# Decoder layer on one core: the two output projections of a chunk in one run of segments, layer-norm sums taken in the residual's addition, pools in another order

## The chip, the cores and the metric

One NeuronCore of a Trainium2 chip runs the whole layer in one launch. The metric is the device time in microseconds (us) of that core, median over runs; less is better. TensorE (PE), VectorE (DVE), ScalarE (ACT), GpSimd (POOL) and SyncE (SP) each execute their own instructions in order. In this program SP issues every DMA.

## The reference

One layer of a decoder, sequence 2048, width 1024, float32. What matters of it here:

```
shift, scale, gate = silu(c) W_ada + b_ada
h = x * (1 + scale) + shift
[q k v | g_attn | u B C | g_conv | m_attn m_conv] = h W_in
A: 3 dilated causal head groups, 4 heads x 128 each, merged per head by
   softmax denominators;      a = (o * silu(g_attn)) W_attn_out
B: s = (B * conv3_causal(C * u) * silu(g_conv)) W_conv_out
y = (sigmoid(m_attn) * a + sigmoid(m_conv) * s) W_o
out = LayerNorm(alpha * x + (1 + gate) * y)        # eps 1e-5, gain, bias
```

## The kernel before

Every product is a float32 product in three matmuls: each operand is split into a high and a low part (ACT casts the high part, L517; DVE subtracts it, L518), and hi·hi, lo·hi and hi·lo are added in one PSUM bank.

**Stage 1** computes the combined projection by Strassen-Winograd block products of seven (L617 to L619), the gates, the short convolution, and writes q, k, gates (`sg_scr`) and the convolution's rows (`y_scr`) to DRAM.

**Stage 2** (`attention_stage`) is a list of segments that a small look-ahead runner (`run_segs`) works through: weights are loaded five segments ahead and split three ahead. Groups g = 1 and 2 come first, then group 0 over four chunks of 512 tokens. In a chunk c of group 0 there are the V products and heads, the merges of the three groups for the four heads (`merge`, L449 to L458, all on DVE: a head's output times a broadcast weight, plus two other groups' outputs times theirs, times a gate; three `ab`, two `og` and one `gt` loads each), `co_segs(c)` (the convolution's output projection: eight segments of 24 matmuls; gate load L318, multiplication L319, store to `pa_scr` L320), and `ao_segs(c - 1)` (the attention's output projection: eight segments of 12 matmuls; gate load L332, load of the stored product L333, multiplication L334, addition L335, store to `mg_scr` L336). `ao_segs(3)` ends the stage. Three PSUM banks (`mm`) hold the products of V and of both projections, so that PE's fourth product in a row waits until DVE has emptied a bank. Both gates' tiles, `sg`, are one pool name with two buffers.

**Stage 3** loads `w_o`, multiplies it by the gate row (L987), forms the seven combinations (T rows), and runs eight steps of two 128-token blocks: load, combine and split the block (L600 to L610, L517, L518), seven products (p1 to p7, 12 matmuls each), and in `put` the residual and the layer norm: addition L1006, `alpha * x` added L1007, an ACT pass for the mean L1012, an ACT pass for the squares L1013, a power on POOL L1015, scaling L1017, gain on DVE L1018, bias on POOL L1019.

The order of the instructions on each engine is decided by a scheduler at build time; waits are put where tiles are shared. Pools are stacked: a pool's memory is reused by a later pool, and the first use waits for what was there.

Of the kernel before, what the change touches and what calls it, by code (L numbers as in the profile page):

```python
# [11 lines left out]
F32 = mybir.dt.float32  # L12
F32R = mybir.dt.float32r
# [19 lines left out]
LAG = 384  # L33
W_Q, W_K, W_G, W_U, W_B, W_C, W_GC, W_MA, W_MC = 0, 12, 24, 28, 36, 44, 52, 60, 68
# [19 lines left out]
def attention_stage(tc, psum1, wp, hp, kq, pa, pm, split, ident, scp, mod, w_v, w_ao, w_co, xm, xn,  # L54
                    qk_scr, nb_scr, ga_scr, o_scr, st_scr, st0_scr, al_scr, om_scr, y_scr, sg_scr, pa_scr, mg_scr):
# [90 lines left out]
    def classes_of(t):  # L146
        return t.rearrange("p (a r) -> p r a", r=4)

    nb = [[kq.tile([P, P if g == 2 else 256], F32, name=f"nb{g % 2}{j}" if g < 2 else f"nb{g}{j}")
           for j in range(NH)] for g in range(3)]  # L150

    def load_nb(g):
        for j in range(NH):
            SP.dma_start(nb[g][j], nb_scr[g, j, :, :256 if g < 2 else P])
# [157 lines left out]
    def co_segs(c):  # L312

        ys, at = [], slice((c % 2) * CH, (c % 2 + 1) * CH)
        for d in range(KT):
            def coseg(i, unit, d=d):
                sg = pm.tile([P, CH], F32, name="sg", bufs=2)
                SP.dma_start(sg, sg_scr[c // 2, 1, d, :, at])  # L318
                V.tensor_mul(sg, sg, gemm(unit, ys))  # L319
                SP.dma_start(pa_scr[c // 2, d, :, at], sg)  # L320
            seg([w_co[d]], coseg, prep_rows([y_scr[c // 2, k, :, at] for k in range(KT)], ys) if d == 0 else None)

    def ao_segs(c):

        os_, at, box = [], slice((c % 2) * CH, (c % 2 + 1) * CH), {}
        for d in range(KT):
            def aoseg(i, *units, d=d):
                if units:
                    box["u"] = units[0]
                sg = pm.tile([P, CH], F32, name="sg", bufs=2)  # L330
                co = pm.tile([P, CH], F32, name="co", bufs=2)
                SP.dma_start(sg, sg_scr[c // 2, 0, d, :, at])  # L332
# [5 lines left out]
            seg([w_ao[d // 2]] if d % 2 == 0 else [], aoseg,  # L338
                prep_rows([om_scr[c, :, j, :] for j in range(NH)], os_) if d == 0 else None)
# [59 lines left out]
    for c in range(NCH):  # L399
# [5 lines left out]
        def done(j, ps, c=c, st=st, o0=o0, box=box):  # L405
# [11 lines left out]
            for g in (1, 2):  # L417
                raw = pm.tile([NH * 4, 2, P], F32, name="alr", bufs=2)
# [52 lines left out]
    for g in (1, 2, 0):  # L471
        load_nb(g)
# [4 lines left out]
def layer_kernel(ctx: ExitStack, tc: tile.TileContext, x, xm, xn, cvec, wada, bada, w_main, w_v,  # L477
# [35 lines left out]
    pa_scr = dram.tile([2, KT, P, PAIR], F32, name="pa_scr")  # L513
# [9 lines left out]
    @contextmanager  # L523
    def block_products():

        with ExitStack() as s:
            rooms["ps"] = s.enter_context(tc.tile_pool(name="psum2", bufs=1, space=bass.MemoryType.PSUM,
                                                       reuse_waits="tile"))
            rooms["work"] = s.enter_context(tc.tile_pool(name="work", bufs=1, reuse_waits="tile"))
            rooms["t"] = s.enter_context(tc.tile_pool(name="tp", bufs=1, reuse_waits="tile"))  # L530
            rooms["s"] = s
            yield rooms["work"]

    def t_pool(i):

        if i < 3:
            return rooms["t"]
        if rooms.get("s3") is not rooms["s"]:
            rooms["s3"] = rooms["s"]
            rooms["t3"] = rooms["s"].enter_context(tc.tile_pool(name="tp3", bufs=1, reuse_waits="tile"))  # L540
        return rooms["t3"]
# [4 lines left out]
    def big():  # L546
        return rooms["work"].tile([P, PAIR + 64], F32, name="big", bufs=4)

    def row():
        return rooms["work"].tile([P, DM], F32, name="row", bufs=2)  # L550

    def half():
        return rooms["work"].tile([P, CH], F32, name="t", bufs=7)

    def raw_tile():
        return rooms["work"].tile([P, DM], F32, name="raw", bufs=3)

    def t_split(T, p, i, src):
        hi = t_pool(i).tile([P, CH], F32R, name=f"th{p}{i}")
        lo = t_pool(i).tile([P, CH], F32R, name=f"tl{p}{i}")  # L560
        split(hi, lo, src)
        T[p, i] = (hi, lo)
# [213 lines left out]
    with block_products() as w:  # L776
# [4 lines left out]
        with tc.tile_pool(name="ada", bufs=1, reuse_waits="tile") as ada:  # L781
# [26 lines left out]
            first_h(3)(xa, xb)  # L808
        t_row(T, 3, xa, xb)
# [151 lines left out]
    with ExitStack() as stage:  # L961
# [3 lines left out]
        wp, hp, kq, pa, pm = (pool(n) for n in ("wp", "hp", "kq", "pa", "pm"))  # L965
        attention_stage(tc, psum1, wp, hp, kq, pa, pm, split, ident, scp, mod, w_v, w_ao, w_co, xm, xn,
                        qk_scr, nb_scr, ga_scr, o_scr, st_scr, st0_scr, al_scr, om_scr, y_scr, sg_scr, pa_scr, mg_scr)

    w = ctx.enter_context(block_products())
# [4 lines left out]
    def load_w(i):  # L974
        def load(xa, xb):
            if i == 0:
                gate_row = rows_["gate"] = row()
                for hh in range(2):
                    pg = ps_bank()
                    for k in range(4):  # L980
                        PE.transpose(pg[:, k * P:(k + 1) * P],
                                     mod[:, 2, hh * 4 + k:hh * 4 + k + 1].to_broadcast([P, P]), ident)
                    S.copy(gate_row[:, hh * CH:(hh + 1) * CH], pg)
# [11 lines left out]
    for tb in range(0, SEQ // P, 2):  # L995
        def norm(tb=tb):
            zs = [big()[:, :DM] for _ in range(2)]

            def put(k, hh, last):
                def f(r, bank):  # L1000
                    z = zs[k]
# [5 lines left out]
                    V.scalar_tensor_tensor(z[:, hs], xr, ALPHA, z[:, hs], op0=ALU.mult, op1=ALU.add)  # L1007
# [6 lines left out]
                    V.tensor_scalar(mv[:, 1:2], mv[:, 1:2], 1.0 / DM, LN_EPS, op0=ALU.mult, op1=ALU.add)  # L1014
# [69 lines left out]
```

## Time and profile before

| | |
|---|---|
| runs | 2724.41, 2720.09, 2718.11 us; median 2720.09 |
| the profiled execution | 2715.16 us, of which the span of the profile is 2713.4 |
| PE busy | 2482.0 us (91%) |
| DVE busy | 1721.0 us (63%) |
| ACT, POOL busy | 1057.3 us (39%), 74.1 us (3%) |
| mean granted TensorE clock | 0.96 of full speed |

Stage 1 lies at 0 to 1533.6 us, groups 1 and 2 at 1533.6 to 1916, group 0 with the projections at 1916 to 2452, stage 3 at 2452 to 2713.4. The busy shares are means over stages with different limits; what a stage loses is read from its waits and its clock, in the rows below.

### The profile page before, as it was taken

How to read it: one execution, taken by the hardware profiler on the slowest of the kernel's cores; microseconds unless marked ns; L12 is line 12 of the kernel's file. 1: busy time of each engine (PE TensorE's matmuls, PEld its weight loads, DVE VectorE, ACT ScalarE, POOL GpSimd, SP SyncE). 2: the span in 40 equal slices, each digit the busy share in tenths (PEclk: the TensorE clock that was granted, in tenths of full speed). 3: DMA queues.
4: the chain of work that ended last, by engine and by line, in shares of the span. 5: the costliest groups of instructions: out<-in, count | busy, mean ns of one | idle time of the engine just before them, and what ended most of it. 6: DMA issues, size and time to landing. Idle time of an engine off the chain costs nothing.

```text
span 2713.4 us, 32007 instructions
## 1 busy us (share of the span) xinstructions
PE 2482.0 (91%) x11878; PEld 2102.1 (77%) x11878; DVE 1721.0 (63%) x2787; ACT 1057.3 (39%) x1741; POOL 74.1 (3%) x46
## 2 busy tenths in 40 slices
PE   3999999999989999999999799999999697956786
PEld 2778888888877888888888699999987586844664
DVE  8745566676667555676655346545677767658665
ACT  5323333333453223333333345554635243303444
POOL 2000000000000000000000000000000000000232
PEclk8999999999999999999999899999999898978888
DMA  6333322212443323122122455544578878675332
GB/s 237 121 111 128 113 70 78 70 67 97 148 163 104 122 101 117 63 70 77 63 101 94 145 150 152 150 116 136 174 245 265 265 244 270 213 241 172 113 117 100
DMA packets 205769, 378.73 MB, mean 140 GB/s; under 512 B 22653, under 2 KB 93484, under 8 KB 205612
## 3 DMA queue, kind: packets, MB, share of 16 engines
q1 hardware_dynamic: 205612, 376.68, 43.2%
q8 instruction: 93, 1.52, 0.2%
q14 instruction: 64, 0.52, 0.1%
HBM read 282.71 MB, written 93.90 MB: 139 GB/s over the span
## 4 chain that ended last, share of the span: by engine, by line
PE 70%; DMA 11%; DVE 9%; issue 6%; ACT 2%; POOL 1%; SPq 1%; POOLq 0%; DVEq 0%; ACTq 0%
PE pb L617 17%; PE pb L619 17%; PE pb L618 17%; PE mm L139 5%; PE mm L140 5%; PE mm L141 5%; DMA sg<-sg_scr 2%; DVE tl L518 1%; DMA ab<-al_scr 1%; DMA og<-o_scr 1%; DMA mg_scr<-sg 1%; DMA xs<-in_xn 1%; PE pt L221 1%; POOL big L1019 1%; DMA kr<-qk_scr 1%
## 5 line engine op out<-in xcount | busy, mean ns | idle before, releaser
L617 PE MATMUL pb<-th,w2h 128*128 128x512 f32 x2016 | 800.0, 399 | 84.0 <-ACT th L517 58.6
L618 PE MATMUL pb<-tl,w2h 128*128 128x512 f32 x2016 | 799.3, 397 | 9.9 <-DVE tl L518 9.8
L619 PE MATMUL pb<-th,w2l 128*128 128x512 f32 x2016 | 797.1, 397 | 12.0 <-DVE w2l L518 12.0
L617 PEld LDWEIGHTS pb<-th,w2h 128*128 128x128 f32 x2016 | 385.7, 191 | 180.6 <-ACT th L517 68.1
L618 PEld LDWEIGHTS pb<-tl,w2h 128*128 128x128 f32 x2016 | 386.2, 192 | 100.4 <-DVE tl L518 20.4
L619 PEld LDWEIGHTS pb<-th,w2l 128*128 128x128 f32 x2016 | 386.8, 192 | 96.1 <-DVE w2l L518 16.0
L517 ACT CAST w2h<-raw 128x1024 fp32r<-128x1024 f32 x168 | 176.7, 1052 | 345.6 <-PE pb L618 285.9
L518 DVE TENSOR_TENSOR w2l<-raw,w2h 128x1024 fp32r<-128x1024 f32 x168 | 214.2, 1275 | 150.0 <-ACT w2h L517 149.8
L626 ACT COPY t<-pb 128x512 f32<-128x512 f32 x248 | 144.3, 584 | 367.7 <-PE pb L619 363.5
L139 PE MATMUL mm<-whi,hhi 128*128 128x256 f32 x768 | 250.6, 327 | 19.4 <-ACT hhi L517 15.9
L141 PE MATMUL mm<-whi,hlo 128*128 128x256 f32 x768 | 247.2, 324 | 2.6 <-DVE hlo L518 2.6
L140 PE MATMUL mm<-wlo,hhi 128*128 128x256 f32 x768 | 248.4, 324 | 0.0
L139 PEld LDWEIGHTS mm<-whi,hhi 128*128 128x128 f32 x768 | 184.9, 241 | 21.3 <-ACT hhi L517 17.4
L139 PE MATMUL mm<-hhi,whi 128*128 128x512 f32 x384 | 158.4, 413 | 45.4 <-DVE sg L334 43.1
L141 PEld LDWEIGHTS mm<-whi,hlo 128*128 128x128 f32 x768 | 184.1, 241 | 3.2 <-DVE hlo L518 3.2
L140 PEld LDWEIGHTS mm<-wlo,hhi 128*128 128x128 f32 x768 | 185.3, 241 | 0.1
L517 ACT CAST whi<-raw 128x1024 fp32r<-128x1024 f32 x96 | 100.6, 1048 | 168.9 <-PE mm L140 70.9
L518 DVE TENSOR_TENSOR wlo<-raw,whi 128x1024 fp32r<-128x1024 f32 x96 | 116.9, 1219 | 69.8 <-ACT whi L517 69.5
L140 PE MATMUL mm<-hlo,whi 128*128 128x512 f32 x384 | 155.4, 405 | 0.2 <-DVE hlo L518 0.2
L141 PE MATMUL mm<-hhi,wlo 128*128 128x512 f32 x384 | 155.3, 405 | 0.0
L517 ACT CAST w2h<-xs 128x1024 fp32r<-128x1024 f32 x84 | 88.6, 1055 | 132.8 <-PE pb L618 114.4
L617 PE MATMUL pb<-th,w1h 128*128 128x512 f32 x336 | 132.6, 395 | 3.5 <-DVE big L1006 3.0
(169 smaller groups left out, 3421.4 us busy)
## 6 DMA issues: line engine op xcount, KB each, us to landing
raw<-in_w_main SPq DMA_DIRECT2D x152, 512.0 KB
qk_scr<-big SPq DMA_DIRECT2D x48, 512.0 KB
raw<-in_w_v SPq DMA_DIRECT2D x48, 512.0 KB
sg_scr<-big SPq DMA_DIRECT2D x32, 512.0 KB
sg<-sg_scr SPq DMA_DIRECT2D x64, 256.0 KB
raw<-in_w_co SPq DMA_DIRECT2D x32, 512.0 KB
qr<-qk_scr SPq DMA_DIRECT2D x48, 256.0 KB
ab<-al_scr SPq DMA_DIRECT2D x48, 256.0 KB
```

Source lines behind the costliest of these rows:

```text
L139: PE.matmul(o, a[0], b[0], start=start, stop=False)
L140: PE.matmul(o, a[0], b[1], start=False, stop=False)
L141: PE.matmul(o, a[1], b[0], start=False, stop=stop)
L221: PE.transpose(ps[:, n * P:(n + 1) * P], P_t[b][:, a:a + P], ident)
L517: S.copy(hi, src)
L518: V.tensor_sub(lo, src, hi.bitcast(F32))
L617: PE.matmul(bank, a[0], b[0], start=start, stop=False, **kw)
L618: PE.matmul(bank, a[0], b[1], start=False, stop=False, **kw)
L619: PE.matmul(bank, a[1], b[0], start=False, stop=stop, **kw)
L626: S.copy(r, bank)
L1019: G.tensor_add(z, z, rows_["b"])
```

## The change

- `out_segs(c)` takes the place of `co_segs` and `ao_segs`: the segments of both projections of one chunk are interleaved, attention's output tile d three behind the convolution's (`LATE = 3`). The convolution's gated product stays in its tile (`sg1`, five buffers) until it is added; `pa_scr` and its 64 transfers are gone. Each gate has its own tile name. `out_segs(c - 1)` follows chunk c's V and heads; `out_segs(3)` ends the stage, so that `out_segs(2)` and `out_segs(3)` are one run.
- Merges come two to a segment. `alr` has one buffer. Group 0's bias tiles share those of group 1 and are loaded later.
- The norm's mean comes from an addition that also sums its row (L1014); the ACT pass for the mean is dropped; the square pass is in two halves, into `half()` tiles; the gate row is scaled by 1/alpha so that x is added unscaled.
- Stage 2's pools are entered as wp, hp, pm, kq, pa, and stage 3's as s, T rows 1 to 3, T row 0, prep.

```diff
-    def co_segs(c):
...
-                V.tensor_mul(sg, sg, gemm(unit, ys))
-                SP.dma_start(pa_scr[c // 2, d, :, at], sg)
...
-    def ao_segs(c):
...
-                SP.dma_start(co, pa_scr[c // 2, d, :, at])
...
+    def out_segs(c):
+        os_, ys, at, box, late = [], [], slice((c % 2) * CH, (c % 2 + 1) * CH), {}, []
         for d in range(KT):
+            def gate(which, d=d):
+                sg = pm.tile([P, CH], F32, name=f"sg{which}", bufs=LATE + 2 if which else 2)
+                SP.dma_start(sg, sg_scr[c // 2, which, d, :, at])
+                return sg
+
+            def coseg(i, unit, d=d, gate=gate):
+                sg = box["co", d] = gate(1)
                 V.tensor_mul(sg, sg, gemm(unit, ys))
...
+            def aoseg(i, *units, d=d, gate=gate):
...
+                sg = gate(0)
                 V.tensor_mul(sg, sg, gemm(box["u"], os_, base=(d % 2) * NH))
-                V.tensor_add(sg, sg, co)
+                V.tensor_add(sg, sg, box["co", d])
...
+            co()
+            late.append(ao)
+            if d >= LATE:
+                late.pop(0)()
+        while late:
+            late.pop(0)()
...
+        if c == 0:
+            after(len(segs), lambda: load_nb(0))
...
-            after(len(segs) + 3 + jj, lambda jj=jj, merge=merge: merge(jj))
+            after(len(segs) + 3 + jj // 2, lambda jj=jj, merge=merge: merge(jj))
         pre_all(first, xn[c], h, None)
-        co_segs(c)
         if c > 0:
-            ao_segs(c - 1)
-    ao_segs(NCH - 1)
+            out_segs(c - 1)
+    out_segs(NCH - 1)
...
-        wp, hp, kq, pa, pm = (pool(n) for n in ("wp", "hp", "kq", "pa", "pm"))
+        wp, hp, pm, kq, pa = (pool(n) for n in ("wp", "hp", "pm", "kq", "pa"))
...
-    w = ctx.enter_context(block_products())
+    w = ctx.enter_context(block_products("s", (1, 2, 3), (0,), "prep"))
...
                     V.tensor_add(z[:, hs], r, bank)
-                    V.scalar_tensor_tensor(z[:, hs], xr, ALPHA, z[:, hs], op0=ALU.mult, op1=ALU.add)
+                    V.tensor_tensor_reduce(z[:, hs], xr, z[:, hs], 1.0, 0.0, ALU.add, ALU.add,
+                                           accum_out=sums[:, hh:hh + 1])
...
-                    o = raw_tile()
-                    S.activation(o, z, AF.Copy, scale=-1.0 / DM, accum_out=mv[:, 0:1])
-                    S.activation(o, z, AF.Square, bias=mv[:, 0:1], accum_out=mv[:, 1:2])
...
+                    V.tensor_add(mv[:, 0:1], sums[:, 0:1], sums[:, 1:2])
+                    V.tensor_scalar(mv[:, 0:1], mv[:, 0:1], -1.0 / DM, 0.0, op0=ALU.mult, op1=ALU.add)
+                    for h2 in range(2):
+                        S.activation(half(), z[:, h2 * CH:(h2 + 1) * CH], AF.Square, bias=mv[:, 0:1],
+                                     accum_out=sums[:, 2 + h2:3 + h2])
```

How the scheduler's order moves is shown at three places. The first is DVE where the merges of chunk 3 stand (`o` a head's output, `ab` a broadcast weight, `og` another group's output, `gt` a gate, `sg` an output gate). Before:

```order
L449 TENSOR_TENSOR o_18975<-o_18975,ab 128x512
L319 TENSOR_TENSOR sg<-sg,mm 128x512
L518 TENSOR_TENSOR wlo<-raw,whi 128x1024
L454 TENSOR_TENSOR ab<-ab,og 128x4x128
L455 TENSOR_TENSOR o_18975<-o_18975,ab 128x512
L454 TENSOR_TENSOR ab<-ab,og 128x4x128
L455 TENSOR_TENSOR o_18975<-o_18975,ab 128x512
L458 TENSOR_TENSOR o_18975<-o_18975,gt 128x512
L449 TENSOR_TENSOR o_19070<-o_19070,ab 128x512
L454 TENSOR_TENSOR ab<-ab,og 128x4x128
L455 TENSOR_TENSOR o_19070<-o_19070,ab 128x512
```

And now, from the first merge of chunk 3 on:

```order
L455 TENSOR_TENSOR o_18506<-o_18506,ab 128x512
L460 TENSOR_TENSOR ab<-ab,og 128x4x128
L461 TENSOR_TENSOR o_18506<-o_18506,ab 128x512
L460 TENSOR_TENSOR ab<-ab,og 128x4x128
L325 TENSOR_TENSOR sg_19027<-sg_19027,mm 128x512
L461 TENSOR_TENSOR o_18506<-o_18506,ab 128x512
L524 TENSOR_TENSOR wlo<-raw,whi 128x1024
L464 TENSOR_TENSOR o_18506<-o_18506,gt 128x512
L455 TENSOR_TENSOR o_18600<-o_18600,ab 128x512
L460 TENSOR_TENSOR ab<-ab,og 128x4x128
L331 TENSOR_TENSOR sg_19061<-sg_19061,mm 128x512
L461 TENSOR_TENSOR o_18600<-o_18600,ab 128x512
```

Before, one multiplication that empties a bank (L319) stands in the second merge and the next (L334) behind the fourth; now there is one in the first merge (L325) and one in the second (L331).

The second place is SP at the end of stage 2, where the gates of the last projections are loaded. Before:

```order
L336 DMA mg_scr<-sg 128x4x128
L332 DMA sg<-sg_scr 128x512
L333 DMA co<-pa_scr 128x512
L64 DMA raw<-in_w_ao 128x1024
L332 DMA sg<-sg_scr 128x512
L336 DMA mg_scr<-sg 128x4x128
L333 DMA co<-pa_scr 128x512
L332 DMA sg<-sg_scr 128x512
```

And now, in `out_segs(3)` (L320 loads a gate of either kind, L333 stores the sum):

```order
L320 DMA sg_19463<-sg_scr 128x512
L65 DMA raw<-in_w_co 128x1024
L333 DMA mg_scr<-sg_19407 128x4x128
L320 DMA sg_19487<-sg_scr 128x512
L320 DMA sg_19517<-sg_scr 128x512
L65 DMA raw<-in_w_ao 128x1024
L333 DMA mg_scr<-sg_19463 128x4x128
L320 DMA sg_19539<-sg_scr 128x512
```

Before, each gate of the attention's projection stands right behind a store of a sum, with 12 matmuls from one to the next; now a store and two loads stand per 36 matmuls.

The third place is ACT in a step of stage 3 (`w2h<-raw` the casts of a block, `mv` and `ss` the norm's sums, `t<-pb` a copy of a bank). Before:

```order
L1012 ACTIVATE raw,mv<-big 128x1024
L517 CAST w1h<-t 128x512
L1013 ACTIVATE raw,mv<-big,mv 128x1024
L1012 ACTIVATE raw,mv<-big 128x1024
L1017 ACTIVATE big<-big,mv 128x1024
L1013 ACTIVATE raw,mv<-big,mv 128x1024
L517 CAST w2h<-raw 128x1024
L1017 ACTIVATE big<-big,mv 128x1024
L517 CAST w2h<-xs 128x1024
```

And now:

```order
L1022 ACTIVATE t,ss_20474<-big,mv 128x512
L523 CAST w1h<-t 128x512
L1022 ACTIVATE t,ss_20474<-big,mv 128x512
L523 CAST w2h<-raw 128x1024
L1028 ACTIVATE big<-big,mv 128x1024
L1022 ACTIVATE t,ss_20473<-big,mv 128x512 x2
L630 COPY t<-pb 128x512
L1028 ACTIVATE big<-big,mv 128x1024
L523 CAST w2h<-raw 128x1024
L630 COPY t<-pb 128x512
L523 CAST w2h<-xs 128x1024
```

Before, the next block's first cast (`w2h<-raw` ahead of `w2h<-xs`) stands ahead of the second block's scaling (L1017); now it stands behind both scalings (L1028). On PE the products of a step are p1, p2, p5, p4 of one step and then p6, p7, p3 of the step before it, so that between p3 and the next first use of that cast 45 matmuls stand, where there were 16.

## Rows read from the trace of the kernel before

**Rows 1.** The page's first line.
```profile
span 2713.4 us, 32007 instructions
```

**Rows 2.** Windows: stretch, its length, busy us and count by engine, PEclk, DMA, GB/s.
```profile
0.00:1533.60 1533.60, 1478.33 (x6414) 1209.43 (x6414) 975.38 (x1375) 561.05 (x747) 16.27 (x14) 0.99 0.31 104
...
1916.00:2452.00 536.00, 453.87 (x2511) 393.64 (x2511) 370.55 (x688) 187.28 (x378) 0.00 (x0) 0.92 0.77 241
2004.70:2160.90 156.20, 123.12 (x666) 105.51 (x665) 117.46 (x219) 56.86 (x120) 0.00 (x0) 0.90 0.82 258
```

**Rows 3.** Waits of PE, 1916 to 2452: us in total, times, longest us.
```profile
PE mm L139 <- DVE sg L334: 46.5, 14, 18.3
PE pt L221 <- ACT p L214: 25.0, 5, 9.7
PE s L139 <- DVE st L212: 7.8, 2, 5.9
```

**Rows 4.** Waits of DVE in the same stretch.
```profile
DVE sg L334 <- DMA sg<-sg_scr: 32.8, 17, 6.5
```

**Rows 5.** Timeline of PE behind a wait: start, us, engine, line; consecutive matmuls between.
```profile
2151.23 0.63 PE L139 MATMUL mm<-hhi,whi 128*128 128x512 f32 x1
...
2153.36 0.63 PE L141 MATMUL mm<-hhi,wlo 128*128 128x512 f32 x1
...
2154.57 0.40 PE L139 MATMUL mm<-hhi,whi 128*128 128x512 f32 x1
...
2157.09 0.39 PE L141 MATMUL mm<-hhi,wlo 128*128 128x512 f32 x1
```

**Rows 6.** DMA of 1916 to 2452, and two of its issues.
```profile
DMA packets 88222, 129.14 MB, mean 241 GB/s; under 512 B 8016, under 2 KB 41872, under 8 KB 88186
...
pa_scr<-sg SPq DMA_DIRECT2D x32, 256.0 KB
co<-pa_scr SPq DMA_DIRECT2D x32, 256.0 KB
```

**Rows 7.** Timeline of DVE: first merge row of chunk 3, first multiplication behind the last.
```profile
2363.94 0.69 DVE L449 TENSOR_TENSOR o<-o,ab 128x512 f32<-128x512 f32 x1
...
2393.05 0.68 DVE L334 TENSOR_TENSOR sg<-sg,mm 128x512 f32<-128x512 f32 x1
```

**Rows 8.** Timeline of SP at the start of stage 2.
```profile
1535.79 4.68 SPq L154 DMA_DIRECT2D nb<-nb_scr  x9
```

**Rows 9.** Timeline of PE: first product of stage 3, its wait in brackets.
```profile
2468.70 0.80 PE L617 MATMUL pb<-th,w2h 128*128 128x512 f32 x1 [15.80 <-ACT th L517]
```

**Rows 10.** Windows of five steps of stage 3: the first, and the line under all.
```profile
2524.69:2551.59 26.90, 22.66 (x86) 17.50 (x87) 18.24 (x22) 12.08 (x17) 7.74 (x5) 0.88 0.37 117
...
sum 135.83, PE 111.91 PEld 86.34 DVE 91.30 ACT 60.63 POOL 38.57; mean PE 22.38 PEld 17.27 DVE 18.26 ACT 12.13 POOL 7.71
```

**Rows 11.** Groups by form in these steps: busy us, mean ns, idle before, releasers.
```profile
L619 PE MATMUL pb<-th,w2l 128*128 128x512 f32 x120 | 52.4, 443 | 8.9 <-DVE w2l L518 8.9
L617 PE MATMUL pb<-th,w2h 128*128 128x512 f32 x121 | 52.0, 436 | 15.4 <-ACT w2h L517 15.4
...
L1019 POOL TENSOR_TENSOR big<-big,row 128x1024 f32<-128x1024 f32 x10 | 28.4, 2838 | 31.0 <-DVE big L1018 16.7 <-DVE mv L1014 14.3
...
L610 DVE TENSOR_TENSOR t<-raw,xs 128x512 f32<-128x512 f32 x5 | 14.4, 2887 | 0.0
...
L1017 ACT ACTIVATE big<-big,mv 128x1024 f32<-128x1024 f32 x10 | 12.4, 1242 | 19.0 <-issue 10.2 <-DVE mv L1016 7.2 <-ACT raw L1012 1.5
L1018 DVE TENSOR_TENSOR big<-big,row 128x1024 f32<-128x1024 f32 x10 | 12.2, 1223 | 6.8 <-ACT big L1017 6.8
L1015 POOL TENSOR_TENSOR mv<-mv,powe 128x1 f32<-128x1 f32 x11 | 12.0, 1086 | 66.3 <-DVE mv L1014 66.3
...
L1012 ACT ACTIVATE raw<-big 128x1024 f32<-128x1024 f32 x10 | 10.6, 1061 | 12.8 <-DVE big L1007 12.8
```

**Rows 12.** Groups of DVE by form, whole span: an operation that also sums its row.
```profile
L212 DVE CUSTOM_DVE_ANT_0 p<-s,nb 128x256 f32<-128x256 f32 x108 | 40.5, 418 | 1.5 <-PE s L141 1.5
```

More of the change, by code (lines that the diff above doesn't have):

```diff
@@ L33 @@
 LAG = 384
+LATE = 3
 W_Q, W_K, W_G, W_U, W_B, W_C, W_GC, W_MA, W_MC = 0, 12, 24, 28, 36, 44, 52, 60, 68
@@ L147, in classes_of @@
         return t.rearrange("p (a r) -> p r a", r=4)
-    nb = [[kq.tile([P, P if g == 2 else 256], F32, name=f"nb{g % 2}{j}" if g < 2 else f"nb{g}{j}")
-           for j in range(NH)] for g in range(3)]
+    nb = [None] * 3
     def load_nb(g):
+        w = P if g == 2 else 256
+        nb[g] = [kq.tile([P, w], F32, name=f"nb{max(g, 1)}{j}") for j in range(NH)]
         for j in range(NH):
-            SP.dma_start(nb[g][j], nb_scr[g, j, :, :256 if g < 2 else P])
+            SP.dma_start(nb[g][j], nb_scr[g, j, :, :w])
     def load_qk(g, j, c, box):
@@ L323, in ao_segs @@
-    def ao_segs(c):
-        os_, at, box = [], slice((c % 2) * CH, (c % 2 + 1) * CH), {}
-        for d in range(KT):
-            def aoseg(i, *units, d=d):
+            def gate(which, d=d):
[4 more added lines that the diff above has]
+                sg = box["co", d] = gate(1)
+                V.tensor_mul(sg, sg, gemm(unit, ys))
@@ L336, in aoseg @@
                 SP.dma_start(mg_scr[c * 4:(c + 1) * 4, :, d, :].rearrange("b q t -> q b t"),
                              sg.rearrange("q (b t) -> q b t", t=P))
-            seg([w_ao[d // 2]] if d % 2 == 0 else [], aoseg,
-                prep_rows([om_scr[c, :, j, :] for j in range(NH)], os_) if d == 0 else None)
+            co = lambda d=d, f=coseg: seg([w_co[d]], f, prep_rows(
+                [y_scr[c // 2, k, :, at] for k in range(KT)], ys) if d == 0 else None)
+            ao = lambda d=d, f=aoseg: seg([w_ao[d // 2]] if d % 2 == 0 else [], f, prep_rows(
+                [om_scr[c, :, j, :] for j in range(NH)], os_) if d == 0 else None)
@@ L417, in done @@
             for g in (1, 2):
-                raw = pm.tile([NH * 4, 2, P], F32, name="alr", bufs=2)
+                raw = pm.tile([NH * 4, 2, P], F32, name="alr", bufs=1)
                 SP.dma_start(raw, st_scr[g - 1, c].rearrange("j k s c n -> (j k) s (c n)"))
@@ L463, in attention_stage @@
         for jj in range(NH):
-            after(len(segs) + 3 + jj, lambda jj=jj, merge=merge: merge(jj))
+            after(len(segs) + 3 + jj // 2, lambda jj=jj, merge=merge: merge(jj))
         pre_all(first, xn[c], h, None)
-        co_segs(c)
         if c > 0:
-            ao_segs(c - 1)
-    ao_segs(NCH - 1)
-    for g in (1, 2, 0):
+            out_segs(c - 1)
+    out_segs(NCH - 1)
+    for g in (1, 2):
         load_nb(g)
@@ L523, in block_products, with open_room @@
     @contextmanager
-    def block_products():
+    def block_products(*order):
         with ExitStack() as s:
+            rooms["stack"] = s
             rooms["ps"] = s.enter_context(tc.tile_pool(name="psum2", bufs=1, space=bass.MemoryType.PSUM,
                                                        reuse_waits="tile"))
[L529 to L541, printed above, removed]
+            for what in order:
+                open_room(what)
+            yield rooms["s"]
+    def open_room(what):
+        name = what if isinstance(what, str) else "t" + "".join(map(str, what))
+        pool = rooms["stack"].enter_context(tc.tile_pool(name=name, bufs=1, reuse_waits="tile"))
+        for key in ((what,) if isinstance(what, str) else what):
+            rooms[key] = pool
     def ps_bank():
@@ L546, in big @@
     def big():
-        return rooms["work"].tile([P, PAIR + 64], F32, name="big", bufs=4)
+        return rooms["prep"].tile([P, PAIR + 64], F32, name="big", bufs=4)
     def row():
-        return rooms["work"].tile([P, DM], F32, name="row", bufs=2)
+        return rooms["prep"].tile([P, DM], F32, name="row", bufs=2)
     def half():
-        return rooms["work"].tile([P, CH], F32, name="t", bufs=7)
+        return rooms["prep"].tile([P, CH], F32, name="t", bufs=7)
     def raw_tile():
-        return rooms["work"].tile([P, DM], F32, name="raw", bufs=3)
+        return rooms["s"].tile([P, DM], F32, name="raw", bufs=3)
     def t_split(T, p, i, src):
-        hi = t_pool(i).tile([P, CH], F32R, name=f"th{p}{i}")
-        lo = t_pool(i).tile([P, CH], F32R, name=f"tl{p}{i}")
+        hi = rooms[i].tile([P, CH], F32R, name=f"th{p}{i}")
+        lo = rooms[i].tile([P, CH], F32R, name=f"tl{p}{i}")
         split(hi, lo, src)
@@ L773, in bias_tiles @@
         return tiles
-    with block_products() as w:
+    with block_products("s", "prep", (0, 1, 2)) as w:
         V.memset(halo, 0.0)
@@ L808, in layer_kernel @@
             first_h(3)(xa, xb)
+        open_room((3,))
         t_row(T, 3, xa, xb)
@@ L997, in norm @@
             zs = [big()[:, :DM] for _ in range(2)]
+            ss = [w.tile([P, 4], F32, name=f"ss{k}", bufs=2) for k in range(2)]
             def put(k, hh, last):
                 def f(r, bank):
-                    z = zs[k]
+                    z, sums = zs[k], ss[k]
                     hs = slice(hh * CH, (hh + 1) * CH)
```

18 lines of the change are left out of this document (5 added, 13 removed).

## The prediction

> **What bounds the kernel now.** I read the page's first line, then the windows by stage, because busy shares over the whole span mix stages. The span is 2713.4 us [rows 1], the execution 2715.2, and the median of the three runs 5 us above that. In stage 1 PE is busy 1478 of 1534 us at a granted clock of 0.99: PE is the limit there, and the change does not touch it. From 1916 to 2452, where group 0, the merges and both projections lie, PE is busy 454 of 536 us at 0.92, DVE 371, and the DMA share is 0.77 [rows 2]. So this stage loses 82 us to waits of PE, and more to a slower clock.
>
> The waits of PE name the losses [rows 3]: 46.5 us for the multiplication L334 that empties a bank in the attention's projection (14 waits), 25.0 and 7.8 in the heads. DVE in turn stood at L334 for 32.8 us because a gate had not come from DRAM [rows 4]. The longest wait, 18.3 us, is of another kind: the four merges of chunk 3 hold DVE from 2363.9 to 2393.05 [rows 7], and L334 stands behind them in order, so that PE has no empty bank. I count the 18.3 as merge, and 46.5 - 18.3 = 28.2 us in 13 waits as gate.
>
> Behind a wait the matmuls run at the lower of the clock's two levels: from 2151.23 to 2153.36 they start 0.43 us apart, from 2154.57 to 2157.09 (11 on) 0.23 [rows 5]. About nine matmuls at +0.2 us make 1.8 us for each wait.
>
> In stage 3 a step takes 135.83 / 5 = 27.2 us, with PE busy 22.4 [rows 10]. Its 84 matmuls at 0.229 would be 19.2. The waits in a step are 15.4 / 5 = 3.1 us for the first cast and 8.9 / 5 = 1.8 for its low part [rows 11].
>
> **The change, term by term.**
>
> A. Start of stage 2. Nine bias loads take 4.68 us of SP [rows 8], 0.52 each; four of them now come later, so the first weights are asked for 2.1 us earlier. Bounds 0 and 3; I take **2**. The four loads come later in SP's order among other loads, for tiles whose last reader (group 1's heads of the last chunk) stands a block of group 2 earlier: nothing, or the same 2 us if a queue stands behind them.
>
> B. The stage of the projections, in four parts.
> Gates: before, each gate load stood behind the store of the sum ahead of it, and 12 matmuls (12 x 0.23 = 2.8 us) had to hide store, load and two DVE operations. Now there are 36 matmuls (8.2 us) between two such points, except in the last three tiles of a run, where nothing of the convolution is left. Longest gate wait of DVE: 6.5 us [rows 4], under 8.2. So I let 28.2 us fall to 8 (the tails; 13 waits to 4): 20 us, and 9 waits' slow clock at 1.8: 16. Together 36; bounds 18 (only half) and 28.2 + 23 = 51.
> Merges: they do the same work on DVE, some 29 us for four. Together they cost 18.3 + 25.0 + 7.8 = 51 us. In the order now an emptying multiplication stands in the first and in the second merge, with work of 12 to 24 matmuls released by each (2.8 to 5.5 us): I take 3 us for each chunk, **12** in all. Bounds 0, and 30 if every bank comes in time.
> New costs: the V segments of chunks 0 and 1 now follow each other with no projection between, so chunk 0's merges are covered only by chunk 1's V and heads; and at each boundary from a projection back to V, or from convolution to attention rows, the splits have a shorter lead. I take the half of one four-merge block uncovered, 15 us, less the cover that chunk 3's projection gains by the run of 16 segments behind it: **-9**, bounds -25 and 0.
> DMA: 32 stores and 32 loads of 256 KB go [rows 6], 16.8 of 129.1 MB. At the 258 GB/s of the densest stretch [rows 2] the remaining 112.4 MB take 436 us, less than the 497 that I forecast for this stage: no term, but no stage under 436.
> Sum of B: 36 + 12 - 9 = **39**, bounds about -7 (18 + 0 - 25) and 81.
>
> C. From stage 2 to 3. PE waits 15.8 us for the first T row [rows 9]: last gates, last sum, `w_o` (loaded now into memory that comes free before the end), product with the gate row. The load is no longer behind the last sums in time, but DVE still has its T rows to form. I take a third, **5**; bounds 2 and 9.
>
> D. Steps of stage 3. The ACT pass L1012 goes (1.06 us, twice a step [rows 11]). The new addition with sum is 512 wide; the one row of such an operation is 0.42 us at 256 wide [rows 12], so between 0.42 and 0.84, four a step in place of four plain additions: 0 to 1.7 us more for DVE a step, I take 0.5, and six tiny ones. DVE's 18.3 us [rows 10] has room under 24.
> What decides is the order. Before, the first cast of the next block waits for p3's row only loosely, and PE has 16 matmuls (3.7 us) from p3 to its first use: the chain from p3 to the cast is thus 3.7 + 3.1 = 6.8 us. Now 45 matmuls (10.3 us) stand there, but the cast stands behind both scalings, so the chain gains the power (1.09), the scaling (1.24), the gain on DVE (1.22) and a bias on POOL ahead of the power (2.84), and loses one pass, 1.06 [rows 11]; the squares in halves give 0.6 back: 6.8 + 1.09 + 1.24 + 1.22 + 2.84 - 1.06 + 0.6 = 12.7. The wait is 12.7 - 10.3 = 2.4 us instead of 3.1. With 1.0 for the low part, which p7 now covers in part, and 1.8 of slow clock for one wait, a step is 19.2 + 2.4 + 1.0 + 1.8 = **24.4 us**, 2.8 less than 27.2; six of the eight steps run so: 6 x 2.8 = **17**. Bounds: 22 us (no wait; then DVE with its 18.3 and the two POOL additions is nearest) gives 31; nothing gained gives 0.
>
> On this term the skill has a rule. The POOL addition takes 2.84 us and DVE's L610, 512 wide, 2.89, while L1018, twice as wide, takes 1.22 [rows 11]: one waits for the other. The Trainium skill (SBUF — State Buffer, Who interferes with whom) states that a DVE operation with two inputs in SBUF and a GpSimd operation that reads SBUF exclude each other wholly; the trace agrees in L610's 2.89 us. By that rule alone the step could not go under DVE's own time plus both additions, 18.3 + 5.7 - 2.2 (L610's excess, already within) = 21.8 us, which is under 24.4 and leaves the sum as it is.
>
> E. The tail behind the last product has the same chain of norm, scaling, gain, bias and store: 0.
>
> Sum: 2 + 39 + 5 + 17 = 63. From the profiled 2715.2 that is 2652, and with the 5 us by which the median lies above, **2657 us**.
>
> **The rivals.**
>
> 1. Everything works out better: gate waits and their clock vanish (51), merges give 30, steps take 22 us (31): 2 + 81 + 5 + 31 = 119, **2601 us**. For it: 36 matmuls over each gate. Against it: three tiles at each run's end without cover, and four merges that are the same DVE work. 0.15.
>
> 2. Both POOL additions come to stand in the chain from p3 to the cast, since DVE is shut out while POOL adds: 12.7 + 2.84 = 15.5, the wait 5.3 us, a step 27.3. Stage 3 gains nothing: 63 - 17 = 46, **2674 us**. For it: L610's 2.89 us. Against it: one of the additions lies under p5 and p4. 0.16.
>
> 3. No change. The merges' waits grow by what the gates give back: B is 0 and D with it: 7 us, **2713 us**. That is within 0.2% (5.4 us), which is about what a measurement of this kernel can tell from no change, or just under. For it: the merges come two to a segment, closer together. 0.05.
>
> 4. Slower. DVE is in order, and if PE's three banks are all filled when the merges begin, each of the four merge blocks stalls PE for its 29 us, 116 instead of 51: -65 in place of +12. Then B is 36 - 65 - 9 = -38, and the sum 2 - 38 + 5 + 17 = -14: **2734 us**. It decides once the merge blocks cost PE over 51 + 36 + 24 - 9 = 102 us. For it: chunk 3's 18.3 us. Against it: in the order now two multiplications stand within the first two merges. 0.07.
>
> **How the numbers follow.** The forecast above holds 0.57, with its own band of 2630 to 2685 (half of B's bounds). The likeliest is 2657. The range 2605 to 2705 holds the forecast, rival 2 and half of rival 1: 0.57 + 0.16 + 0.08 = 0.81. Faster by over 0.2%: forecast, 1 and 2, 0.88; within: 0.05; slower: 0.07.
>
> **What would show it.** Right: in the stage of the projections the waits for the attention's multiplication fall from 46.5 to under 25 us with most of them in merges and run ends, no wait of DVE for a gate outside the last three tiles of a run, granted clock 0.94 or more, PE's waits in the heads near 30. In stage 3 steps of 24 to 25 us, a wait for the first cast of 2 to 3 us, the mean clock above 0.88. The first product of stage 3 waits some 11 us instead of 15.8. Wrong: merges of over 25 us without a matmul at each chunk (rival 4), steps of 27 us with DVE rows of 2.8 us beside POOL's additions (rival 2), or gate loads that still come last (rival 3). What I trust least is B's term for the merges, since DVE's order within a merge and the arrival of three kinds of loads decide it together.

## The result and the profile after

The changed kernel takes 2681.98 us (median of four runs, 2677.93 to 2683.97), before 2722.25 in the same comparison: ratio 0.985, 95% interval 0.9828 to 0.9871. The forecast was 2657 in a range of 2605 to 2705: faster, as forecast, by 40 us instead of 63. The profiled execution fell by 2713.4 - 2676.1 = 37.3 us of span, and that is what the rows can divide.

The first lines of the page after, against [rows 1]:

```profile
span 2676.1 us, 31985 instructions
...
PE 2468.6 (92%) x11878; PEld 2091.5 (78%) x11878; DVE 1727.0 (65%) x2867; ACT 1043.8 (39%) x1741; POOL 66.4 (2%) x46
```

The windows of the changed kernel, cut at its own borders (columns as in [rows 2]): the stage of the projections, and stage 3 in all.

```profile
1915.90:2424.00 508.10, 447.99 (x2510) 390.71 (x2508) 368.00 (x690) 185.84 (x378) 0.00 (x0) 0.93 0.73 225
2424.00:2676.10 252.10, 178.90 (x680) 130.77 (x680) 188.77 (x314) 101.46 (x164) 50.27 (x32) 0.88 0.36 116
```

Group 0 begins at 1915.9 us in both kernels, so the start of stage 2 gave nothing in the end. The stage of the projections is 28 us shorter (536.1 to 508.1), stage 3 is 9.3 us shorter (261.4 to 252.1).

The waits of PE in the stage of the projections after, against [rows 3], and of DVE for a gate, against [rows 4]:

```profile
PE mm L140 <- DVE sg L331: 21.5, 4, 10.5
PE ot L140 <- DVE o L413: 10.1, 2, 6.1
PE pt L223 <- ACT p L216: 8.8, 1, 8.8
PE mm L140 <- DVE sg L325: 8.1, 3, 3.8
```

(Before, the convolution's multiplication had one such wait:)

```profile
PE mm L139 <- DVE sg L319: 2.0, 1, 2.0
```

```profile
DVE sg L331 <- DMA sg<-sg_scr: 5.0, 2, 2.7
```

Fourteen waits for the attention's multiplication have become four; with the convolution's, 15 waits of 48.5 us have become 7 of 29.6. DVE waits 5.0 us for a gate instead of 32.8. Most of what is left lies in the merges. PE's idle time while DVE works through the four merge blocks was 7.4, 15.2, 12.5 and 17.7 us before, 52.7 in all; after it is 11.2, 13.3, 11.1 and 10.3, 45.8 in all. (These are the gaps between PE's matmuls, added up from each block's first merge instruction to its last and cut off there.) Outside the merges it fell from 82.1 - 52.7 = 29 to 60.1 - 45.8 = 14 us. PE's busy time fell by 5.9.

Chunk 3's merges on DVE show what remains, beside [rows 7] (start, us, line, operation; the gap of PE behind them is the last row):

```profile
2331.42 0.69 DVE L331 TENSOR_TENSOR sg<-sg,mm 128x512 f32<-128x512 f32 x1
...
2336.60 0.68 DVE L325 TENSOR_TENSOR sg<-sg,mm 128x512 f32<-128x512 f32 x1
...
2338.17 0.68 DVE L331 TENSOR_TENSOR sg<-sg,mm 128x512 f32<-128x512 f32 x1
...
2349.89 0.69 DVE L464 TENSOR_TENSOR o<-o,gt 128x512 f32<-128x512 f32 x1
2352.87 0.69 DVE L331 TENSOR_TENSOR sg<-sg,mm 128x512 f32<-128x512 f32 x1 [2.29 <-DMA sg<-sg_scr]
```

```profile
2353.71 0.77 PE L140 MATMUL mm<-hhi,whi 128*128 128x512 f32 x1 [10.55 <-DVE sg L331]
```

Several multiplications that empty a bank now lie within the first three merges. The fourth still has none, and behind it a gate arrives 2.29 us late, so PE stands for 10.55 us where it stood for 18.3.

In stage 3, three regular steps in a row, from the first product p1 of one to that of the next, against [rows 10]:

```profile
2530.12:2555.04 24.92, 21.69 (x85) 16.69 (x85) 19.51 (x33) 10.43 (x18) 6.53 (x4) 0.93 0.41 126
2555.04:2579.39 24.35, 20.40 (x85) 15.48 (x85) 19.63 (x33) 10.53 (x18) 6.58 (x4) 1.00 0.40 131
2579.39:2603.77 24.38, 20.39 (x84) 15.47 (x84) 19.64 (x33) 10.52 (x18) 6.26 (x4) 1.00 0.34 109
```

And groups by form in these steps, against [rows 11]:

```profile
L621 PE MATMUL pb<-th,w2h 128*128 128x512 f32 x72 | 29.8, 414 | 9.7 <-ACT w2h L523 7.8 <-ACT t L630 1.9
L623 PE MATMUL pb<-th,w2l 128*128 128x512 f32 x72 | 29.0, 405 | 1.5 <-DVE w2l L524 1.5
...
L614 DVE TENSOR_TENSOR t<-raw,xs 128x512 f32<-128x512 f32 x3 | 8.5, 2837 | 0.0
L1014 DVE CUSTOM_DVE_ANT_0 big<-t,big 128x512 f32<-128x512 f32 x12 | 8.0, 687 | 0.8 <-DMA t<-in_x 0.8
```

A step is 24.4 us (24.9 in the first, part of which ran at the lower level of the clock), with a wait of 7.8 / 3 = 2.6 us for the first cast, 0.5 for its low part and 0.6 for a copy. But stage 3 gained only 9.3 us. The same windows in three parts (from the last projection to the third step's first product; five steps; from the last step's first product to the end), before and after:

```profile
2452.00:2522.00 70.00, 42.55 (x142) 27.68 (x140) 59.84 (x88) 32.05 (x49) 1.36 (x2) 0.83 0.49 160
2522.00:2657.80 135.80, 111.42 (x420) 85.94 (x420) 91.27 (x111) 60.63 (x85) 38.54 (x21) 0.87 0.36 116
2657.80:2713.40 55.60, 32.45 (x120) 24.61 (x120) 28.77 (x38) 21.03 (x30) 17.94 (x11) 0.79 0.28 95
```

```profile
2424.00:2487.80 63.80, 42.07 (x140) 27.49 (x141) 57.70 (x86) 26.48 (x40) 0.00 (x0) 0.81 0.43 136
2487.80:2603.80 116.00, 98.70 (x398) 75.34 (x396) 90.58 (x152) 51.02 (x83) 30.06 (x19) 0.97 0.38 120
2603.80:2676.10 72.30, 38.13 (x144) 27.94 (x144) 40.49 (x78) 23.95 (x42) 20.22 (x13) 0.79 0.27 91
```

The first two parts are 26 us shorter, the last is 16.7 us longer. 24 matmuls more are left for the last part (about 5.5 us at 0.23); the other 11 are waits without cover, nearly all one wait:

```profile
2644.23 0.79 PE L621 MATMUL pb<-th,w2h 128*128 128x512 f32 x1 [10.48 <-ACT t L630]
```

```profile
2642.91 0.71 ACT L1022 ACTIVATE t<-big,mv 128x512 f32<-128x512 f32 x1
2643.52 0.19 ACT L1022 ACTIVATION_READ_ACCUMULATOR t<-big,mv 128x1 f32 x1
2643.61 0.56 ACT L630 COPY t<-pb 128x512 f32<-128x512 f32 x1
```

The last p6 needs a copy of its bank, and the copy stands on ACT behind the squares of both blocks of the step before. In the middle, products of the next steps cover this; at the end there are none.

### The profile page after: what moved, and what is told of

Same layout as the page of the kernel before. It is cut to its first block, busy times and chain, and to the rows that moved or that the text cites. A ratio compares the mean times of both kernels' runs of the same rounds, so it can differ in the third digit from the quotient of the medians.

```text
span 2676.1 us, 31985 instructions
## 1 busy us (share of the span) xinstructions
PE 2468.6 (92%) x11878; PEld 2091.5 (78%) x11878; DVE 1727.0 (65%) x2867; ACT 1043.8 (39%) x1741; POOL 66.4 (2%) x46
```

## The experiments

All runs were compared with runs of the kernel before on the same chip. The two stage lengths come from each kernel's own profile (group 0's first matmul to the last matmul of a projection; from there to the end). Kernels in which a stage is the same differ by 2 to 3 us in it (505.7 to 508.9 and 260.5 to 262.4). The runs come from several chips, so that rows are best compared by their ratios.

| kernel | median us | ratio to before, 95% interval | projections us | stage 3 us |
|---|---|---|---|---|
| before | | 1 | 536.1 | 261.4 |
| changed | 2682.0 | 0.9850 (0.9828 to 0.9871) | 508.1 | 252.1 |
| e1 projections alone | 2682.2 | 0.9876 (0.9857 to 0.9896) | 505.9 | 260.5 |
| e2 norm alone | 2709.3 | 0.9970 (0.9959 to 0.9982) | 535.7 | 251.7 |
| e3 pools alone | 2720.4 | 1.0012 (1.0000 to 1.0024) | 536.6 | 262.4 |
| e4 changed, old norm | 2682.8 | 0.9877 (0.9858 to 0.9896) | 508.6 | 260.5 |
| e5 product through DRAM | 2703.0 | 0.9951 (0.9934 to 0.9967) | 533.4 | 250.9 |
| e6 the same, not interleaved | 2708.6 | 0.9963 (0.9949 to 0.9978) | 535.1 | 256.8 |
| e7 merges three segments apart | 2681.0 | 0.9865 (0.9847 to 0.9884) | 511.6 | 252.1 |
| e9 last copies on DVE | 2674.3 | 0.9840 (0.9821 to 0.9858) | 505.7 | 249.8 |
| e10 64 copies more | 2676.8 | 0.9844 (0.9827 to 0.9861) | 506.0 | 251.6 |
| e11 stores alone | 2686.0 | 0.9885 (0.9866 to 0.9904) | 521.4 | 249.9 |
| e12 gate row in stage 1 | 2666.2 | 0.9809 (0.9791 to 0.9827) | 508.9 | 239.8 |
| e13 DRAM, more gate tiles | 2700.9 | 0.9938 (0.9924 to 0.9952) | 529.9 | 251.1 |

**Which part brought what (e1 to e4).** The change was taken apart: the attention stage alone, the norm alone, the pools' orders alone, and everything but the norm. The edits are shortened to the lines that tell the runs apart.

```diff
 e1  -        co_segs(c) ... ao_segs(c - 1)
     +        out_segs(c - 1)          # with merges, alr and nb as changed
 e2  -        V.scalar_tensor_tensor(z[:, hs], xr, ALPHA, z[:, hs], ...)
     +        V.tensor_tensor_reduce(z[:, hs], xr, z[:, hs], ...)
 e3  -        ("wp", "hp", "kq", "pa", "pm")
     +        ("wp", "hp", "pm", "kq", "pa")
 e4  e1 + e3
```

> Only the output projections, merges and bias tiles of the change; stage 3 and all pool orders as before. Theory (the 28 us that the stage of the projections lost come from the order of its segments alone): that stage 508 us instead of 536, stage 3 unchanged at 261 us, time about 28 us under before (2694, ratio 0.990). Rival (part of it comes from pools that come free earlier): stage 515 to 525 us, time 2700 to 2712.

> Only the layer norm of the change. Theory (the norm's edit changes the order of the products, steps fall from 27.2 to about 24.4 us, and the products put off to the end cost most of it): steps 24 to 25 us, a wait of some 10 us for a copy in front of the last p6, total 2 to 5 us under before. Rival (the order comes from the pools, the norm alone saves one pass a block off the path): steps 27 us, order as before, total within 2 us of before.

> Only the pools' orders of the change. Theory: the first product of stage 3 comes 4 to 6 us earlier behind the last projection, the T rows end where they ended before because DVE forms them, total 0 to 2 us under before. Rival (the earlier w_o is worth what the first product shows): 5 to 6 us under before.

> The changed kernel with the layer norm of before. Theory: steps of 27 us again and no products put off to the end, so 3 to 9 us slower than the changed kernel: 2685 to 2691. Rival (the norm's edit costs as much at the end as it brings in the steps): the same as the changed kernel within 3 us, or faster.

The windows of the stage of the projections and of stage 3 with the projections alone, and of stage 3 with the norm alone:

```profile
1914.50:2420.40 505.90, 449.83 (x2510) 393.76 (x2508) 368.01 (x690) 185.99 (x378) 0.00 (x0) 0.93 0.71 221
2420.40:2680.90 260.50, 184.50 (x681) 136.63 (x680) 178.57 (x234) 113.78 (x164) 57.88 (x32) 0.85 0.36 120
```

```profile
2454.40:2706.10 251.70, 178.24 (x680) 130.43 (x678) 190.70 (x315) 101.01 (x164) 50.56 (x32) 0.89 0.37 127
```

In e1 the attention stage's edit alone has the whole gain of its stage (30 us, ratio 0.9876, more than the 0.990 expected); that it is the order alone which brings it, e1 does not show. The norm alone has the whole gain of stage 3: steps of 24.4 to 24.7 us and a wait of 10.38 us in front of the last p6. By the median it brought more than the 2 to 5 us expected, 8. The pools alone bring nothing (ratio 1.0012), and their first product did not come 4 to 6 us earlier as expected: it came 18.9 us behind the last projection, 16.7 before. In e4, with the old norm, the changed pools leave stage 3 at 260.5, and by the ratios e4 is 7 us slower than the changed kernel, within the 3 to 9 expected. The parts add up: 0.9876, 0.9970 and 1.0012 multiplied give 0.9858, against 0.985.

**Why the projections became faster (e5, e6).** The product goes through DRAM again, first with the interleave kept, then without it (`LATE = 8`).

```diff
 e5  -                sg = box["co", d] = gate(1)
     +                sg = gate(1)                 # two buffers for each gate
                      V.tensor_mul(sg, sg, gemm(unit, ys))
     +                SP.dma_start(pa_scr[c // 2, d, :, at], sg)
 ...
     +                SP.dma_start(co, pa_scr[c // 2, d, :, at])
     -                V.tensor_add(sg, sg, box["co", d])
     +                V.tensor_add(sg, sg, co)
 e6  -LATE = 3
     +LATE = 8
```

> The changed kernel, but the convolution's gated product goes through DRAM again (32 stores, 32 loads of 256 KB), with the interleaved order kept. Theory (the gain is the order, which puts 36 matmuls over each gate): the stage of the projections stays at 508 to 513 us, total within 5 us of the changed kernel. Rival (the traffic or the round trip itself was the cost): 16.8 MB at 225 to 258 GB/s are 65 to 75 us of transfers, of which 10 to 25 us show: 2692 to 2707.

> As the kernel before it in this call (product through DRAM), and the interleave is undone too: eight convolution segments, then eight of attention, with separate gate tiles of two buffers each, merges two to a segment. Theory: gate waits of DVE are back at 25 to 33 us, the stage at 525 to 537 us, total 2697 to 2710. Rival (the shared gate buffers or the new place of the projections behind V were what mattered): within 5 us of the kernel before it.

The window of the stage in e5, and its waits of PE:

```profile
1915.10:2448.50 533.40, 454.26 (x2510) 393.98 (x2508) 370.85 (x690) 185.72 (x378) 0.00 (x0) 0.92 0.79 247
```

```profile
PE mm L140 <- DVE sg L334: 34.0, 5, 19.3
PE mm L140 <- ACT hhi L527: 15.3, 6, 7.4
PE ot L140 <- DVE o L416: 9.3, 3, 5.6
```

My theory fell. With the interleave but the product in DRAM, the stage is 533.4 us, 2.7 under before: nearly all of the gain is gone. DVE does wait less for gates (of both kinds 14.9 us in e5, 35.3 in e6, 32.8 before), but PE then waits in other places: 38.6 us for a bank (29.6 in the changed kernel), of which 19.3 and 13.7 us at two merge blocks, and 15.3 us for split rows (`hhi`) that come late (4.5). Undoing the interleave as well (e6) costs the stage 1.7 us more, which is within the differences of equal stages; its total is 3 to 6 us above that of e5, most of which lies in stage 3 (256.8 against 250.9), where e6 has no edit. So with the interleave kept, the gain hangs on the round trip. The interleave is what lets the product stay on chip with five tiles; what the product on chip would bring without it, with a tile for each of the eight, no run shows.

**Which part of the round trip (e10, e11, e13).** Copies inside DRAM that nobody waits for; the stores alone; the whole trip with four tiles for the convolution's gate instead of two, and one for the returning product instead of two.

```diff
 e10 +                SP.dma_start(dup[0][c // 2, d, :, at], sg_scr[c // 2, 1, d, :, at])
 e11 +                SP.dma_start(pa_scr[c // 2, d, :, at], sg)      # sum still from the tile
 e13 e5, and
     -                sg = pm.tile([P, CH], F32, name=f"sg{which}", bufs=2)
     +                sg = pm.tile([P, CH], F32, name=f"sg{which}", bufs=LATE + 1 if which else 2)
     -                co = pm.tile([P, CH], F32, name="co", bufs=2)
     +                co = pm.tile([P, CH], F32, name="co", bufs=1)
```

> The changed kernel with 64 more transfers of 256 KB at the places where the product's stores and loads stood: copies inside DRAM that nothing waits for and that wait for no engine. Theory one (the traffic itself was the cost: 16.8 MB on queues that are busy 0.73 of the time): the stage of the projections goes from 508 to 525 to 535 us, total 2697 to 2710. Theory two (SP is in order, and a store that waits for DVE's product holds up the loads behind it, those of the merges too): stage 508 to 514 us, total within 6 us of the changed kernel.

> The changed kernel with the 32 stores of the convolution's gated product issued again on SP, each waiting for DVE's product, but no loads of it: the sum is still taken from the tile. Theory two (the waiting store holds up SP): most of the 25 us are back, stage 523 to 533 us, total 2695 to 2707. Theory one (traffic): half of the bytes, half of the 25 us: 2690 to 2696. Theory three (the load of the product behind its store, and the buffers that both hold, were the cost): within 5 us of the changed kernel.

> The changed kernel with the product's round trip through DRAM, as in the run with 64 transfers, but with four tiles for the convolution's gate instead of two (one for the returning product instead of two). There SP stood 22.0 us at gate loads, 11 times, until a store of the product had left its tile. Theory (the round trip costs by that: a tile is held until its store has landed, and SP waits for it in front of all other loads): those waits are gone, stage 518 to 524 us, as with the stores alone, total 2684 to 2692. Rival (the returning load, behind its store in SP's order and in front of the addition, is the cost): stage 529 to 536 us, total 2697 to 2705.

In e10 the premise failed. The issues of DMA up to 1600 us, in that run:

```profile
dup<-sg_scr SPq DMA_DIRECT2D x64, 256.0 KB
```

All 64 copies were issued before 1600 us, 60 of them in stage 1, because nothing held them back. So the run shows only that 16.8 MB there cost nothing; traffic among the projections it did not test.

In e11 the stores without the loads cost 4 us by the medians, but the kernel before was itself 4.8 us slower beside the changed kernel than beside e11 (2722.3 and 2717.5); by the ratios (0.9885 to 0.9850) they cost 9.5, and beside e10, which ran on the same chip with its projections as in the changed kernel, 9.2. Its profiled execution lay 7 us over its median, so its stage of 521.4 us is on the long side. A cost of 9 us is at the lower end of what theory one expected (8 to 14 us over the changed kernel), above theory three's, and not at theory two's. In e13 SP's waits for a product to leave its tile fell to less than half:

```profile
SPq L320 <- DMA pa_scr<-sg: 22.0, 11, 4.1
```

```profile
SPq L320 <- DMA pa_scr<-sg: 9.2, 5, 3.9
```

(e5 above, e13 below.) The stage stayed at 529.9 us and the total within 2 us of e5, as the rival expected. For the single tile of the returning product SP shows no wait on DVE; at that load it waited 5.9 us for the store. So the held tiles are at most a small part of the cost. The loads that return, with what they do to the other loads, have the larger part by the totals: 14 us (e13 against e11) to 18 (e5 against e11). By the profiled stages they have 8.5 to 12 us, about half.

The bytes moved in the stage, in the changed kernel, e11 and e5:

```profile
DMA packets 80362, 114.14 MB, mean 225 GB/s; under 512 B 7104, under 2 KB 41472, under 8 KB 80327
DMA packets 84951, 122.46 MB, mean 235 GB/s; under 512 B 7616, under 2 KB 41984, under 8 KB 84915
DMA packets 89989, 131.63 MB, mean 247 GB/s; under 512 B 8176, under 2 KB 42544, under 8 KB 89953
```

With 8.3 MB more the stage is 13.3 us longer, with 17.5 MB more 25.3 us: it grows about as its bytes do. That is what theory one says, and it stays open. But in these runs the bytes and the transfers' places in SP's order change together, so it is not shown which of the two costs.

**The merges (e7).**

```diff
-            after(len(segs) + 3 + jj // 2, ...)
+            after(len(segs) + 3 + (jj // 2 if c == 0 else 3 * jj), ...)
```

> The changed kernel with the merges of chunks 1 to 3 three segments apart instead of two to a segment. Theory (bursts of merges keep PE's three banks full, 10 us at a time): the waits of 8.9 to 10.6 us at three places fall under 4 us each, stage 490 to 498 us, 10 to 18 us faster than the changed kernel. Rival (each merge waits for its own loads and costs the same wherever it stands): within 4 us.

The total moved by 1 us. The blocks stayed blocks. In chunk 3 of that run, the first instruction of the first merge and the last of the last:

```profile
2327.78 0.69 DVE L455 TENSOR_TENSOR o<-o,ab 128x512 f32<-128x512 f32 x1 [5.00 <-DMA ab<-al_scr]
...
2359.15 0.69 DVE L464 TENSOR_TENSOR o<-o,gt 128x512 f32<-128x512 f32 x1
```

They are 32.1 us for four merges, 29.7 before the edit: the scheduler put them next to each other again. (The blocks of chunks 1 and 2 are 36.9 and 34.5 us, 32.3 and 32.6 before the edit.) So the run does not say what spread merges would bring, and that is open.

**The end of stage 3 (e9) and its start (e12).**

```diff
 e9  -        S.copy(r, bank)
     +        (V.tensor_copy if last_step else S.copy)(r, bank)
 e12 (on top of e9, in stage 1, once for each of eight row blocks)
     +        SP.dma_start(t[:, hh * CH:(hh + 1) * CH], w_o[...])
     +        V.tensor_mul(t, t, rows_gate[0])
     +        SP.dma_start(wg_scr[k], t)
     (in stage 3)
     -                V.tensor_mul(t[:, :DM], t[:, :DM], rows_["gate"])
     +                SP.dma_start(t[:, :DM], wg_scr[k])
```

> The changed kernel with the three copies of a bank in the last step of stage 3 on DVE instead of ACT. Theory (the first of these copies stands behind the squares of the block before on ACT, and so PE waits 10.5 us in front of the last p6): that wait falls to 3 to 5 us, 5 to 7 us faster than the changed kernel. Rival (DVE stands in the same chain of the norm, in order): within 2 us.

> The changed kernel with the last step's copies on DVE and with the output weights multiplied by the gate row in stage 1, where DVE has idle time, and loaded ready in stage 3. Theory (the T rows at the start of stage 3 are DVE's time, so that earlier weights alone brought nothing there): eight multiplications of 1.17 us leave the stretch from the last projection to the second step's first product, 51 us become 42 to 45, total 6 to 9 us under the kernel with only the copies moved: 2665 to 2669. Rival (that stretch waits for the last sums and their loads): within 3 us of it.

In e9 the wait in front of the last p6 is 8.97 us instead of 10.48. First PE, then DVE:

```profile
2638.32 0.80 PE L621 MATMUL pb<-th,w2h 128*128 128x512 f32 x1 [8.97 <-DVE t L632]
```

```profile
2637.59 0.68 DVE L632 COPY t<-pb 128x512 f32<-128x512 f32 x1
```

The rival was right: on DVE the copy stands behind the same chain of the first block's norm (its last instruction before the copy is of the second block's sums, at 2637.52). Stage 3 fell by 2.3 us, and the ratio cannot be told from the changed kernel's. In e12 the theory held. From the last projection to the second step's first product it is 41.0 us, 50.0 in e9; to the third step's:

```profile
2424.70:2480.80 56.10, 40.22 (x134) 28.03 (x134) 50.32 (x82) 25.11 (x39) 0.00 (x0) 0.79 0.41 136
```

These are 56.1 us, 65.6 in e9 and 63.8 in the changed kernel: DVE sets that stretch, and eight multiplications less shorten it by about their own time (9.6 us of DVE in e9). e12 is the fastest version run, 0.9809 of before.

## Why the prediction was right or wrong

The direction was right, and the total fell into the range. Part of that is luck: the largest term came from transfers that I had put at nothing, and within the steps two errors cancelled.

**A, start of stage 2, 2 us: right, then given back.** The first matmul came at 1546.4 us instead of 1548.5. I had not asked whether what follows would keep the lead. It was lost within 30 us, in two waits that the kernel before does not have:

```profile
1556.64 0.50 PE L140 MATMUL s<-kh,qh 128*128 128x256 f32 x2 [1.03 <-ACT kh L523]
1561.63 0.39 PE L140 MATMUL mm<-whi,hhi 128*128 128x256 f32 x1 [0.86 <-ACT hhi L523]
```

**B, the projections, 39 us: 28 to 30, and the mechanism failed.** "No term" for DMA was the wrong step, and "36 matmuls over each gate" alone was not the reason: e5 keeps those 36 matmuls and gains 2.7 us. My rows were not wrong: DVE's wait for gates was 32.8 us. But as long as the product's 64 transfers stood among them, removing that wait let the next ones through: rows for the splits that come late, and longer waits for a bank. (The merges' own loads are not the difference: DVE waited 29.1 us for them in e5 and 27.7 in the changed kernel.) Of the parts, idle time of PE outside the merges fell by 15 (gates 20 less new costs 9 had been the forecast: 11), the merges by 7 (forecast 12), and busy time by 6, where I had put 16 for the slower clock. The clock term is the one most off in size. I had read one wait [rows 5] and given 1.8 us to all 13 gate waits; by the clock records of the trace only seven of them were followed by the lower level. In all, the lower level lasted 81.9 us of the stage before and 71.7 after; at half speed those 10.2 us are worth 5.1 us, near the 5.9 by which busy time fell. Whether the transfers cost by their bytes or by their place in SP's order is not settled: e10 missed its test, e13 speaks against the held tiles, and in e11 half of the bytes brought back a third of the cost by the ratios and half by the stages.

**C, 5 us: the first product came 6.2 us earlier, and nothing stayed.** One step later 1 us of it was left (the second step's first product stood 50.9 us behind the last projection before, 49.9 after). Between e1 and e4, which differ in the pools, the first product moved from 16.6 to 10.0 us, the second step's from 50.5 to 49.4, and stage 3 is 260.5 us in both. The stretch is DVE's, as I had half said ("DVE still has its T rows to form"), and I should have drawn the conclusion; e12 shows it from the other side.

**D, the steps, 17 us: the step right, the count wrong.** Forecast 24.4 us, measured 24.4; wait for the cast 2.4, measured 2.6. Two errors cancelled within it: no slow clock (1.8 forecast; the granted clock is 1.00 in two of the three steps), but 20.4 us of busy PE instead of 19.2. The chain to the cast is also not the one that I worked out. I had put a bias on POOL ahead of the power. But POOL was idle in front of that power and waited for DVE, where the sum of the second block's squares (L1024) stood behind L614, which began just after the bias:

```profile
2571.49 2.38 POOL L1030 TENSOR_TENSOR big<-big,row 128x1024 f32<-128x1024 f32 x1 [3.81 <-DVE mv L1019]
2576.02 0.86 POOL L1026 TENSOR_TENSOR mv<-mv,powe 128x1 f32<-128x1 f32 x1 [2.15 <-DVE mv L1025]
```

```profile
2571.58 2.84 DVE L614 TENSOR_TENSOR t<-raw,xs 128x512 f32<-128x512 f32 x1
...
2575.06 0.15 DVE L1024 TENSOR_TENSOR mv<-ss 128x1 f32<-128x1 f32 x1
```

"Six of the eight steps" failed: the order that gives these steps defers products, and the last step pays for them.

**E, the tail, 0: the last 18 us behind the last product are as before (17.4), but ahead of it are 10.5 us that I did not see.** I had the order of PE in hand, with p6, p7 and p3 of a step behind the next step's products, and asked what it covers in the middle, not what it leaves bare at the end.

**Rivals.** Rival 2 named the lock between DVE and POOL, and it stands in the chain: L614 takes 2.84 us in these steps (median of all its 84 instructions 0.69). The squares' sums were read by 2573.2, and L1024 came at 2575.06, so some 1.8 of the 2.6 us for the cast are the lock's, by my estimate; no run tests it. What rival 2 expected beyond that did not come, since the step is still 24.4. The floor of 21.8 us in the prediction took all of DVE's time as shut out; that is too much, for L1020, with one input, ran its 0.15 us inside a POOL addition (at 2642.00, POOL from 2641.97 to 2644.32). Rival 4 (merges of 29 us each without a matmul) did not come: 10 to 13 us of idle PE in each block.

## What to carry to other kernels

A wait that ends last in a profile may have another close behind it: price the removal of a wait by what is late next, and test it by removing the wait alone (here the interleave without the on-chip sum gave 3 of 28 us). When an order defers products to cover a wait, price the last iteration as well. A lead at the start of a stretch that another engine bounds was worth nothing here; taking work off that engine was worth its own time (e12).

## What the runs showed of the hardware

The addition that also sums its row takes 0.69 us at 512 columns and 0.08 to read the sum; the operation that it replaced (L1007) took 0.69. But beside a POOL addition of 2.36 us it took 2.69, in the timelines of POOL and DVE of the changed kernel:

```profile
2648.08 2.36 POOL L1030 TENSOR_TENSOR big<-big,row 128x1024 f32<-128x1024 f32 x1 [2.86 <-DVE big L1029]
```

```profile
2648.30 2.69 DVE L1014 CUSTOM_DVE_ANT_0 big<-t,big 128x512 f32<-128x512 f32 x1 [0.30 <-DMA t<-in_x]
```

That is what the Trainium skill says of two inputs in SBUF (SBUF — State Buffer, Who interferes with whom), and the trace agrees for this operation too. In stage 3 one wait of PE of 2.59 us was followed by the lower level of the clock (0.93 granted over that step), and two of 2.58 and 2.57 us were not (1.00 over both). Of the 13 gate waits among the projections before, the seven that were followed by it lasted 2.3 to 3.5 us, the other six 0.2 to 2.3 us.
